# Later tables and a later row transpose in a mixture of 32 expert jobs on one core

## The chip, the cores and the metric

The kernel runs on one core of a Trainium2 chip. Its time is the device time of one execution in microseconds; the times of before are the median and the spread of three runs. Four engines matter here: TensorE (PE, matmuls), VectorE (DVE), ScalarE (ACT) and GpSimd (POOL, which here only issues indirect DMAs); SP issues the weight loads.

## The reference, cut to what matters

One encoder layer over 2048 tokens of 1024 floats: attention and retention share one input and one output projection, and then a mixture of 32 SwiGLU experts follows, of which each token uses two. Only the mixture is touched by the change:

```python
expert_id = grp[:, None] * MOE_EXPERTS_PER_GROUP + top_idx
...
h = jax.nn.silu(xblk @ w_gate[e]) * (xblk @ w_up[e])
return h @ w_down[e]
...
y = jnp.zeros((T + 1, D), f32).at[buf_tok].add(yb.astype(f32) * buf_w[:, None])[:T]
```

Every expert has a list of the tokens that chose it. A list may be longer than the space that the kernel gives it; then the rest has to be computed too.

## The kernel before, in words

Attention, retention, the output projection and the routing fill the first 1264 us. Routing sorts the experts by the length of their lists. Then 32 jobs follow, one for each expert, numbered here from 0. Jobs 0, 1 and 2 are light: a list of up to 128 rows. From job 3 on heavy jobs (128 rows and 32 or 64 more, the overflow of a long list) and light ones alternate, up to the last few.

A job has two parts. `gate_up` (lines 1559 to 1585) multiplies the job's rows by two weight matrices, in eight pieces of 128 x 1024 floats: four quarters q, each with a gate and an up piece. `down` multiplies the result by four more pieces. The weights are float32, and matmuls run on pairs of rounded parts: for each piece `fetch` (line 1469) takes the raw tile `mr` that SP loaded (512 KB, nine buffers), ACT makes the upper part `mh` (line 1484) and DVE the lower part `ml` (line 1485, raw minus upper). There are eight buffers of each part. A light job needs three matmuls of 512 columns for each 128 x 512 half of a piece, so 48 for `gate_up` and 24 for `down`; a heavy one needs two more for each three.

The rows of a job come by indirect DMAs on POOL's queue (`gather`, line 1502; tile `xg`, two buffers, four DMAs for 128 rows; `xgo` for the overflow), two jobs ahead. `rows` (line 1519) turns them: for all but jobs 0 and 31 by a DVE transpose (`turned`, line 1550; tile `xT`, line 1554), from which ACT makes `xhi` (line 1556) and DVE `xlo` (line 1557). `hidden` (line 1588) transposes a job's result on PE (line 1594) and splits it into `hhi` and `hlo`, for `down`.

The order in the source: while `gate_up` of job n runs, `between(q)` is called behind each of its four quarters. There the next side step is taken (q 0, 1 and 3), `hidden` of job n-1 is written down at q 1, the gathers of job n+2 at q 0, the rows of job n+1 at q 2. `down` of job n-1 comes behind `gate_up` of job n. A planner reads this order as priorities and fixes each engine's queue by its own simulated times; an instruction waits in its queue behind all before it. `high_priority` raises a block's priority, `issue_after` puts a block behind a named instruction on that engine's queue.

The side steps are the generators `units` (line 1247) and `completion` (line 1323), 21 steps in all, three in each job from job `SIDE` on. `units` makes the tables that are needed if a list overflows even its own overflow space: small DVE operations (tiles `u_...`), joined by a few small PE matmuls (lines 1260, 1282, 1287, 1294, 1316), each of which takes one of two PSUM buffers `pt`, as `hidden` does. `completion` makes the order in which finished tokens are normalized and stored (tiles `c_...`, `perm`); the first use of `perm` is in `loads` for job 11, called in job 13. The tables of `units` are read behind the last job.

Of the kernel before, what the change touches and what calls it, by code (L numbers as in the profile page):

```python
# [1443 lines left out]
R0 = 0.1  # L1444
W0 = 0.6
DG = 2
SIDE = 1
SQ = (0, 1, 3)
SP = 100
ORD = 1  # L1450
# [223 lines left out]
def experts(k):  # L1674
    nc, tc = k.nc, k.tc
    with ExitStack() as ctx:
        m = Moe(k, ctx)
        f = Final(k, ctx)
        order = job_order()
        jobs = []  # L1680
# [23 lines left out]
        def loads(n):  # L1704
            for c in range(NB):
                if DONE[c] == n:
                    C[c] = f.load(k.perm[:, c:c + 1])

        def column(n, step):

            for c in range(NB):
                if DONE[c] == n:
                    if step == 0:
                        with tc.issue_after(m.hi_at.ins):
                            f.square(C[c])
                    elif step == 1:
                        with tc.issue_after(m.lo_at.ins):
                            f.scale(C[c])
                    else:
                        f.store(C[c])  # L1720

        for n, X in enumerate(jobs):
            def between(q):
                if n >= SIDE and q in SQ:
                    with tc.high_priority(SP):
                        next(side, None)
                if q < 3:
                    if q and n < 31:
                        column(n - 3, q - 1)
                    elif n == 31:  # L1730
                        if q == 1:
                            loads(29)
                        column(28, q)
                if n == 31 and q == 1:
                    m.down(jobs[30], f.loads)
                    C[15] = f.load(k.perm[:, 15:16])
                    C[14] = f.load(k.perm[:, 14:15])
                elif n and q == (1 if n < 31 else 0):
                    with tc.high_priority(HID):
                        m.hidden(jobs[n - 1])  # L1740
                if q == 0:
                    for j in ([1, 2] if n == 0 else [n + 2]):
                        if j < 32:
                            m.gather(jobs[j])
                if q == 2 and n + 1 < 32:
                    if n < 31:
                        loads(n - 2)
                    if n:
                        m.rows(jobs[n + 1])
                    else:  # L1750
                        with tc.issue_after(k.split0.ins):
                            m.rows(jobs[1])
                if q == 3 and n < 31:
                    column(n - 3, 2)
            m.gate_up(X, between)
            if 0 < n < 31:
                m.down(jobs[n - 1], f.loads)
# [9 lines left out]
        n = nc.values_load(k.redo[0:1, 0:1], min_val=0, max_val=1)  # L1767
        with tc.For_i(0, n, 1):
# [3 lines left out]
            n = nc.values_load(k.nu[0:1, 0:1], min_val=0, max_val=64)  # L1772
# [154 lines left out]
```

## Time and profile before

| | us |
|---|---|
| median of three runs | 2099.15 |
| lowest and highest run | 2093.79, 2099.17 |
| profiled execution | 2083.01 |
| its span | 2081.2 |
| mean granted clock of PE | 0.969 |

The profiled execution is one run; between its span and its own time lie 1.8 us. It is 16.1 us (0.8%) below the median. Engine shares are of the span. Times in the rows count from the start of the span.

### The profile page before, as it was taken

The page shows a single profiled execution, that of the slowest core. Times are in us where ns is not written, and L with a number is a line of the kernel's source. Part 1 is how long each engine was busy: PE and PEld are TensorE (multiplying, and loading weights), DVE is VectorE, ACT ScalarE, POOL GpSimd, SP SyncE. Part 2 cuts the span into 40 slices and gives each one's busy share as a digit, 9 for nine tenths or more (in the row PEclk, how much of TensorE's full clock was granted, in tenths as well). Part 3 has the DMA queues.
Part 4 walks back from the last instruction along what each step waited for, and adds up shares of the span by engine and source line. Part 5 has one row for each costly group of instructions (what it writes and reads, how often), then busy time and mean ns, then how long its engine had stood idle before and what let it go on. Part 6 is the DMA issues. An engine that isn't in the chain of part 4 may idle for free.

```text
span 2081.2 us, 30110 instructions
## 1 busy us (share of the span) xinstructions
PE 1944.9 (93%) x9811; PEld 1543.9 (74%) x9811; DVE 1553.2 (75%) x3462; ACT 1122.7 (54%) x1915; POOL 673.7 (32%) x362
## 2 busy tenths in 40 slices
PE   7999999999999987789999996799999999999994
PEld 5788888878888875578887775577777677777673
DVE  7345446855565578987877767999988899998884
ACT  4244445634444454555454314676776787776663
POOL 0000000010000037421111105566867667875433
PEclk9999999999999998899999997799999999999997
DMA  6655344573675456463453455799999999998994
GB/s 201 193 153 171 117 135 144 178 242 129 195 213 167 137 160 215 128 203 132 156 183 111 138 223 182 254 304 296 338 343 320 319 339 349 353 344 302 338 316 117
DMA packets 241810, 459.61 MB, mean 221 GB/s; under 512 B 27376, under 2 KB 130160, under 8 KB 240624
## 3 DMA queue, kind: packets, MB, share of 16 engines
q1 hardware_dynamic: 224384, 401.53, 56.9%
q0 software_dynamic: 16976, 55.06, 9.8%
q8 instruction: 78, 1.28, 0.3%
q10 hardware_dynamic: 288, 1.05, 0.1%
q14 instruction: 84, 0.69, 0.1%
HBM read 365.81 MB, written 91.75 MB: 220 GB/s over the span
## 4 chain that ended last, share of the span: by engine, by line
PE 72%; DVE 9%; DMA 7%; issue 5%; SPq 2%; POOL 2%; ACT 2%; ACTq 0%; DVEq 0%; POOLq 0%
PE pa L63 7%; PE pa L62 7%; PE pa L64 7%; PE acc L63 7%; PE acc L62 7%; PE acc L64 7%; PE acc L72 4%; PE acc L74 3%; PE pS L350 3%; PE pS L351 3%; PE pT L382 2%; PE pF L62 2%; PE pF L64 2%; PE pF L63 2%; DMA wr<-in_w_in_dram 2%
## 5 line engine op out<-in xcount | busy, mean ns | idle before, releaser
L1485 DVE TENSOR_TENSOR ml<-mr,mh 128x1024 fp32r<-128x1024 f32 x376 | 446.5, 1214 | 38.6 <-ACT mh L1484 32.4
L1484 ACT ACTIVATE mh<-mr 128x1024 fp32r<-128x1024 f32 x376 | 385.5, 1055 | 124.0 <-PE acc L74 66.3
L1515 POOL DMA_INDIRECT xg<-XN,TA x120 | 270.0, 2250 | 64.3 <-issue 30.5
L352 DVE CUSTOM_DVE_ANT_0 p<-pS,dist 128x512 f32<-128x512 f32 (+1 forms) x320 | 188.0, 605 | 126.3 <-PE pS L351 118.5
L426 POOL TENSOR_TENSOR U<-U,r 128x512 f32<-128x512 f32 (+2 forms) x13 | 16.5, 1270 | 725.9 <-DVE r L40 623.9
L359 ACT ACTIVATE p<-p,nm 128x128 f32<-128x128 f32 (+15 forms) x128 | 153.9, 1203 | 111.8 <-DVE nm L358 111.5
L63 PE MATMUL acc<-ml,xhi 128*128 128x512 f32 x512 | 205.9, 403 | 5.0 <-DVE ml L1485 5.0
L64 PE MATMUL acc<-mh,xlo 128*128 128x512 f32 x512 | 206.2, 403 | 1.3 <-DVE xlo L1557 1.3
L62 PE MATMUL acc<-mh,xhi 128*128 128x512 f32 x512 | 204.0, 401 | 0.0
L54 ACT ACTIVATE ah<-pT 128x512 fp32r<-128x512 f32 (+2 forms) x176 | 85.4, 498 | 141.1 <-PE pT L382 99.6
L62 PE MATMUL pa<-xh,whi 128*128 128x512 f32 x384 | 152.9, 398 | 2.0 <-DVE nlam L633 2.0
L62 PE MATMUL pa<-whi,xh 128*128 128x512 f32 x384 | 151.8, 398 | 2.9 <-ACT whi L161 2.1
L63 PE MATMUL pa<-wlo,xh 128*128 128x512 f32 x384 | 153.1, 399 | 1.5 <-DVE nm L358 1.2
L64 PE MATMUL pa<-whi,xl 128*128 128x512 f32 x384 | 153.9, 401 | 0.0
L63 PE MATMUL pa<-xl,whi 128*128 128x512 f32 x384 | 151.8, 395 | 0.0
L64 PE MATMUL pa<-xh,wlo 128*128 128x512 f32 x384 | 151.6, 395 | 0.0
L350 PE MATMUL pS<-kst,qs 128*128 128x512 f32 (+1 forms) x320 | 123.5, 398 | 21.6 <-DVE cm L352 8.9
L162 DVE TENSOR_TENSOR wlo<-wr,whi 128x1024 fp32r<-128x1024 f32 x72 | 89.9, 1250 | 67.0 <-ACT whi L161 64.4
L55 DVE TENSOR_TENSOR al<-pT,ah 128x512 fp32r<-128x512 f32 (+2 forms) x176 | 97.5, 564 | 44.9 <-ACT ah L54 44.4
L62 PEld LDWEIGHTS acc<-mh,xhi 128*128 128x128 f32 x512 | 97.3, 190 | 31.8 <-ACT xhi L54 0.2
L161 ACT ACTIVATE whi<-wr 128x1024 fp32r<-128x1024 f32 x72 | 76.1, 1059 | 81.2 <-DMA wr<-in_w_in_dram 39.9
L63 PEld LDWEIGHTS acc<-ml,xhi 128*128 128x128 f32 x512 | 97.6, 191 | 28.9 <-DVE ml L1485 5.4
(536 smaller groups left out, 4912.5 us busy)
## 6 DMA issues: line engine op xcount, KB each, us to landing
mr<-in_expert_w_gate_dram SPq DMA_DIRECT2D x128, 512.0 KB
mr<-in_expert_w_up_dram SPq DMA_DIRECT2D x128, 512.0 KB
mr<-in_expert_w_down_dram SPq DMA_DIRECT2D x128, 512.0 KB
wr<-in_w_in_dram SPq DMA_DIRECT2D x72, 512.0 KB
vst<-VS SPq DMA_DIRECT2D x72, 256.0 KB
qs<-QS SPq DMA_DIRECT2D x128, 128.0 KB
st<-in_x_dram SPq DMA_DIRECT2D x16, 512.0 KB
VS<-st SPq DMA_DIRECT2D x32, 256.0 KB
```

The costliest lines, as they stand in the source:

```text
L54: nc.scalar.activation(hi, ps, AF.Copy)
L55: return nc.vector.tensor_sub(lo, ps, hi.bitcast(F32))
L62: nc.tensor.matmul(out, s_hi, m_hi, start=start, stop=False)
L63: nc.tensor.matmul(out, s_hi, m_lo, start=False, stop=False)
L64: nc.tensor.matmul(out, s_lo, m_hi, start=False, stop=stop)
L162: nc.vector.tensor_sub(lo, r, hi.bitcast(F32))
L350: nc.tensor.matmul(x, qs[0][:, m, 0, o:o + 128], ks[m][:, a0:a1], start=True, stop=False)
L352: nc.vector.tensor_tensor_reduce(p[:, a0:a1], x, tab[:, c0 + a0:c0 + a1], SLOPES[h], -3.0e38, OP.add, OP.max, accum_out=cm[:, n:n + 1])
L359: nc.scalar.activation(p[:, :nk], p[:, :nk], AF.Exp, bias=nm, accum_out=s0 if m == 0 else s1)
L1484: self.hi_at = nc.scalar.activation(hi, r, AF.Copy)
L1485: self.lo_at = nc.vector.tensor_sub(lo, r, hi.bitcast(F32))
L1515: nc.gpsimd.indirect_dma_start(out=xg[:, g * 256:(g + 1) * 256], out_offset=None, in_=v, in_offset=bass.IndirectOffsetOnAxis(ap=ix[:, g], ...
```

## The change

Two things move. The first side step is taken in job 3 and not in job 1; the 21 steps then end in job 9 and not in job 7. The rows of job 2 are written down behind the last quarter of job 1 and not behind its third, and all of that block stands behind `m.lo_at`, the DVE subtraction of the last weight piece that `gate_up` of job 1 fetched. The `loads` keep their place.

```diff
-SIDE = 1
+SIDE = 3
...
-                if q == 2 and n + 1 < 32:
-                    if n < 31:
-                        loads(n - 2)
-                    if n:
+                if q == 2 and n < 31:
+                    loads(n - 2)
+                if q == (3 if n == 1 else 2) and n + 1 < 32:
+                    if n == 1:
+                        with tc.issue_after(m.lo_at.ins):
+                            m.rows(jobs[2])
+                    elif n:
                         m.rows(jobs[n + 1])
```

## Rows read from the trace of the kernel before

**Rows 1.** The profile's page: busy time of each engine with its share of the span and its instructions, and the clock that PE was granted in 40 equal slices of 52 us, in tenths.

```profile
PE 1944.9 (93%) x9811; PEld 1543.9 (74%) x9811; DVE 1553.2 (75%) x3462; ACT 1122.7 (54%) x1915; POOL 673.7 (32%) x362
...
PEclk9999999999999998899999997799999999999997
```

**Rows 2.** PE in order of time: start, length, instruction, count, in brackets the idle time before it and what ended it. The last three lines are the end of `down` of job 1 and the first matmul of job 3.

```profile
1296.82 0.63 PE L62 MATMUL acc<-mh,xhi 128*128 128x512 f32 x2
1302.46 0.79 PE L63 MATMUL acc<-ml,xhi 128*128 128x512 f32 x1 [5.01 <-DVE ml L1485]
...
1306.03 0.63 PE L63 MATMUL acc<-ml,xhi 128*128 128x512 f32 x1
1306.46 0.63 PE L64 MATMUL acc<-mh,xlo 128*128 128x512 f32 x1
1317.90 0.60 PE L1282 MATMUL pt<-u_tri,u_w 32*128 32x32 f32 x2 [10.81 <-DVE u_w L1291]
...
1347.08 0.40 PE L63 MATMUL acc<-ml,hhi 128*128 128x512 f32 x1
1347.32 0.39 PE L64 MATMUL acc<-mh,hlo 128*128 128x512 f32 x1
1347.55 0.39 PE L62 MATMUL acc<-mh,xhi 128*128 128x512 f32 x1
```

**Rows 3.** Waits of all engines from 1325 us to the end: who waited for whom; us in total, times, longest.

```profile
ACT mh L1484 <- PE acc L74: 66.3, 55, 2.8
...
DVE fh L1620 <- DMA fh<-H,perm: 5.8, 1, 5.8
...
PE acc L63 <- DVE ml L1485: 3.7, 5, 1.8
```

**Rows 4.** Stretches: from and to, length, busy us (instructions) of each engine, granted clock of PE as a share of 2.4 GHz, DMA share, GB/s.

```profile
1290.00:1297.00 7.00, 7.00 (x31) 5.64 (x30) 2.15 (x2) 3.26 (x4) 5.52 (x4) 1.00 1.03 404
1297.50:1302.40 4.90, 0.00 (x0) 0.00 (x0) 3.16 (x4) 1.12 (x2) 2.31 (x3) 0.86 0.49 171
1302.40:1307.10 4.70, 4.63 (x10) 3.14 (x10) 4.70 (x7) 4.70 (x6) 4.09 (x3) 0.50 0.77 235
1307.10:1317.90 10.80, 0.00 (x0) 0.03 (x1) 10.80 (x14) 2.45 (x3) 9.89 (x4) 0.50 0.72 222
1317.90:1324.70 6.80, 6.67 (x19) 5.18 (x20) 5.12 (x12) 1.23 (x2) 5.28 (x6) 0.50 0.59 208
1324.70:1347.50 22.80, 22.80 (x99) 17.54 (x98) 19.62 (x31) 18.45 (x21) 5.89 (x5) 1.00 0.85 270
1347.50:1436.00 88.50, 88.28 (x403) 66.69 (x402) 84.58 (x118) 63.79 (x77) 53.66 (x21) 1.00 0.92 306
1480.00:1525.00 45.00, 45.00 (x201) 34.89 (x200) 40.71 (x40) 33.09 (x41) 34.94 (x13) 1.00 0.99 332
```

**Rows 5.** DVE in order of time, with the columns of rows 2.

```profile
1289.82 2.34 DVE L1485 TENSOR_TENSOR ml<-mr,mh 128x1024 fp32r<-128x1024 f32 x2
1299.24 2.01 DVE L1554 STREAM_TRANSPOSE xT<-xg 128x1024 f32<-128x1024 f32 x1 [7.08 <-DMA xg<-XN,TA]
...
1301.20 3.47 DVE L1485 TENSOR_TENSOR ml<-mr,mh 128x1024 fp32r<-128x1024 f32 x3
1304.60 0.13 DVE L1273 CAST u_ui<-u_u 32x1 int32<-32x1 f32 x1
...
1317.55 0.21 DVE L1279 COPY u_w<-u_u 32x128 f32<-32x128 f32 x1
...
1320.37 2.05 DVE L1554 STREAM_TRANSPOSE xT<-xg 128x1024 f32<-128x1024 f32 x1
```

**Rows 6.** DVE from 1264 to 1480 us, grouped by line and operation: count, busy us, mean ns of one, idle time before and its releaser. The last two are the largest and the smallest of the 72 groups of side steps (lines 1260 to 1429); the 72 come to 23.7 us.

```profile
L1554 DVE STREAM_TRANSPOSE xT<-xg 128x1024 f32<-128x1024 f32 x10 | 21.9, 2190 | 7.1 <-DMA xg<-XN,TA 7.1
L1557 DVE TENSOR_TENSOR xlo<-xT,xhi 128x1024 fp32r<-128x1024 f32 x9 | 10.9, 1210 | 0.0
...
L1596 DVE TENSOR_TENSOR hlo<-pt,hhi 128x512 fp32r<-128x512 f32 x8 | 5.4, 677 | 0.0
L1576 DVE SCALAR_TENSOR_TENSOR sg<-sg,wa,acc 128x512 f32<-128x512 f32 x7 | 5.1, 734 | 0.0
L1554 DVE STREAM_TRANSPOSE xT<-xgo 128x512 f32<-128x512 f32 x4 | 4.8, 1191 | 0.0
...
L1557 DVE TENSOR_TENSOR xov<-xT,xov 128x512 fp32r<-128x512 f32 x4 | 2.7, 685 | 0.1
...
L1406 DVE TENSOR_SCALAR c_sl<-i,c_d 128x128 bf16<-128x128 f32 x16 | 3.4, 278 | 0.0
...
L1334 DVE DVE_READ_ACCUMULATOR c_px<-P,posr 32x1 f32 x1 | 0.1, 70 | 0.0
```

**Rows 7.** POOL in order of time: start and length of what issues one gather DMA of a quarter of a job's rows. The second is the last of job 2.

```profile
1283.50 6.49 POOL L1515 DMA_INDIRECT xg<-XN,TA  x1 [0.30 <-issue]
...
1293.29 0.95 POOL L1515 DMA_INDIRECT xg<-XN,TA  x1 [0.30 <-issue]
...
1305.80 5.50 POOL L1515 DMA_INDIRECT xg<-XN,TA  x1 [0.31 <-issue]
```

**Rows 8.** Waits of SP's queue from 1255 us on, with the columns of rows 3.

```profile
SPq L1499 <- DVE ml L1485: 395.5, 264, 9.7
```

## The prediction

> **What bounds the kernel now.** I read the page first: PE is busy 93% of the span, and its clock row falls to 0.7 in the slices 25 and 26, from 1249 to 1353 us [rows 1]. That is where the jobs begin, and there the change works. Then PE in order of time. In the last quarter of job 1 it stands for 5.01 us on the lower part of a weight piece, runs the ten matmuls that are left, and stands for 10.81 us in front of line 1282, a matmul of the second side step [rows 2]. From 1325 us to the end it waits only 3.7 us for weights in all, and it is ACT that waits for PE to give a buffer back, 66.3 us [rows 3]: eight split pieces are normally ready ahead. So past 1325 us a microsecond won on PE is a microsecond of the kernel, as long as DVE and the transfers keep up.
>
> The stretches give the price of the two stops. PE is idle for 4.90 and 10.80 us in them, and after each it runs at half clock (0.50, that is 1.2 GHz) for 4.63 and 6.67 busy us before it is back at 2.4 GHz [rows 4].
>
> DVE in order of time says why it stood. Behind the sixth piece of job 1 its queue has the transpose of job 2's rows, and that waits 7.08 us for a gather; the last two pieces of job 1 stand behind it, though their upper parts are there. The second stop: the copy `u_w`, which line 1282 reads, comes at 1317.55, at the end of a row of tiny side operations with weight pieces between them [rows 5].
>
> **The change part by part.** All sums are made against the profiled execution: 2083.01 us, which is 16.1 below the median of the runs. What is won is subtracted from the median.
>
> *The transpose moved behind the last piece.* The two pieces that PE waits for go ahead of it: DVE is free at 1289.82 + 2.34 = 1292.16, a piece takes 1.13 (three from 1301.20 to 1304.60), so they are there at 1294.4 [rows 5], before PE asks for them at 1297.45. The stop of 5.01 goes [rows 2]. What is late next: the transpose still waits for the gather. Nothing of the gather moves, so I let it begin at 1299.24 again; it takes 1.93, and the first piece of job 0's `down` behind it is ready at 1299.24 + 1.93 + 1.13 = 1302.3. PE ends job 1 at 1297.45 + 10 x 0.235 = 1299.8 (0.235 is the spacing at 1347.08, 1347.32 and 1347.55; at half clock it is 0.43) [rows 2]. Two matmuls of the upper part can go ahead, 0.5, so PE still stands 2.1 here. If the planner puts that piece ahead of the transpose, it is 0; if the gather lands later, it is that much more.
>
> *The side steps moved two jobs.* Line 1282 is no longer in PE's queue in front of `hidden` of job 0: the 10.81 goes. With both stops the half clock goes too, half of 4.63 + 6.67 = 5.6 [rows 4]. The small PE matmuls (lines 1282 to 1316) cost the same two jobs later, so nothing is won on them.
> Gross: 5.0 + 10.8 + 5.6 = 21.4.
>
> *What DVE gives back before job 3.* In the second stop DVE was busy for all of 10.80 us [rows 4]; it worked ahead while PE stood. Without the stop it is the limit. From 1299.24 to the first piece of job 3 it has to do: the transpose 1.93; 16 pieces (4 of job 0's `down`, 8 of job 2, 4 of job 1's `down`) at 1.13, 18.1; `xlo` 1.1; two each of `sg` and `hlo`, 2.5; the rows of job 3, 1.9 + 1.1 + 1.1 + 0.6 with the overflow; the first piece of job 3, 1.1 [rows 5, 6]. That is 29.4: job 3 begins at 1328.6. PE for its part needs from 1302.3 on 24 + 48 + 24 matmuls less the two, 94 x 0.235 = 22.1, and two groups of `hidden` transposes, 0.9: 1325.3. So DVE costs 3.3 more. It is 0 if the rows of job 3 come when DVE is not short, and 5.4 if the planner takes the rows of job 4 ahead as it does now (2.05 at 1320.37) [rows 5]. Cross-check: job 3 begins at 1347.55 now; 18.9 earlier, of which some 2 are side matmuls only moved, agrees with 21.4 - 2.1 - 3.3 = 16.0 to within one.
>
> *What DVE gives back after it.* Now job 3 begins with eight pieces in hand; then it begins with one. From 1347.5 to 1436 DVE is busy 84.58 of 88.5, with side steps in it, and at 1480, when they are over, 40.71 of 45 [rows 4]. The side steps come to 23.7 us of DVE [rows 6]. Moved, jobs 3 to 6 get the first 12 of 21 steps, the light ones, and jobs 7 to 9 the rest. So DVE has a few us to spare in jobs 3 to 6 and is short in 7 to 9. PE loses between 0 (the reserve is built again) and 8 x 1.13 = 9.0 (it was needed whole); I take 3.5, nearer to 0 because the stretch has 3.9 to spare even with the side steps of now.
>
> *The issue_after.* It is a place in a queue, no instruction. What stands behind the transpose on DVE is `down` of job 0, counted above. On ACT `xhi` of job 2 waits with it, and the upper parts behind it; ACT has 1.12 busy of 4.90 there [rows 4], so it is not the later one. SP's queue waits for DVE to free raw tiles (395.5 us over the jobs) [rows 8], so two loads are issued 9 us sooner, behind the two pieces that go ahead; POOL gets buffers back at the same time as now. `loads` keep their place.
>
> Sum: 21.4 - 2.1 - 3.3 - 3.5 = 12.5. Profiled: 2083.0 - 12.5 = 2070.5; median: 2099.15 - 12.5 = **2086.6 us**.
>
> A rule against it: POOL took 0.95 for the last gather DMA of job 2, while DVE stood still, but 6.49 and 5.50 for others beside a busy DVE [rows 7]. In the changed kernel DVE subtracts until 1294.4, across that issue at 1293.29. The Trainium skill, "SBUF — State Buffer", section "Who interferes with whom", says that a DVE instruction with two inputs in SBUF contends with a GpSimd instruction that reads SBUF, and that the loser blocks for the whole instruction; it infers that writing descriptors does not suffer. The long issues here speak for the first, the inference for nothing lost. By the first the gather lands up to two subtractions, 2.3 us, later, and the sum would be 10.2 and 2088.9; by the inference it stays at 12.5.
>
> **The rivals.**
> *Nothing given back.* The planner finds another order, DVE does the pieces of `down` while it waits for the gather, the reserve comes back. For it: 4.8 us of DVE stand idle between 1294.4 and 1299.24, room for four pieces. Against: rows come ahead of `down` in the source. Gain 21.4 less up to 2: 19.5, 2079.6.
> *The transfers are the bound.* From 1297.5 to 1347.5 about 11.9 MB were moved (GB/s times length of the five stretches); at the 332 GB/s that the later jobs reach at a share of 0.99 [rows 4] this takes 35.9 us and not the 33 that I need, and with no raw tiles in hand nothing is left for later. Gain 50 - 35.9 - 2 (moved matmuls) - 9.0 (whole reserve) = 3.1, 2096.0. For it: shares near 1. Against: 404 GB/s were reached from 1290 to 1297, and the loads wait for buffers, not the other way [rows 4, 8].
> *Slower: gathers late at three jobs.* DVE's long busy time stretches POOL's issues (5.50) [rows 7], so the rows of jobs 3 and 4 land after DVE comes to them, too, and each stops PE as now: 3 x (5.0 + 2.3 of half clock) for jobs 2 to 4, and the whole reserve of 9.0 gone: 21.4 - 21.9 - 9.0 = -9.5, 2108.6. It decides if DVE waits for `xg` in three jobs. Against: after 1325 us DVE waits for no gather of rows, the one DMA wait it has is for `fh` [rows 3].
> *It doesn't do what it says.* If the planner still puts job 2's transpose where a needed piece stands behind it (now a piece of `down`) and wins only the side steps, it is the second stop alone: 10.8 + 3.3 - 3.3 - 3.5 = 7.3, 2091.9. This lies inside the range.
>
> **How the numbers follow.** My forecast, gain 7 to 17 (2082 to 2092): 0.55, the last rival within it. Nothing given back: 0.15. Transfers the bound or the reserve lost, gain 0 to 7: 0.21. Slower than now: 0.09. The runs of before spread by 5.4 us; 0.3% is 6.3 us, about what a measurement of this kernel can tell from no change. Faster by more than that: 0.55 + 0.15 + 0.03 = 0.73; within it 0.20; slower by more 0.07. The range takes in the first rival with the spread of the runs, 2077, and most of the second, 2098.
>
> **What would show it.** Right: no wait for line 1282; the pieces of job 1 at 1294.4 and job 2's transpose behind them, still with a DMA wait of some 5 us; PE at 1.00 from 1300 to 1330; job 3 at 1327 to 1332. DVE near 100% until job 9, and PE waits for `ml` there of 2 to 6 us. Wrong: half clock again behind a stop in front of `down` of job 0; a DVE wait for `xg` in job 3 or 4; job 3 at 1335 or later; or PE waits for `ml` above 9 us in jobs 3 to 9.

## The result and the profile after

| | before | after |
|---|---|---|
| median, us (5 runs each, beside each other) | 2093.79 | 2081.85 |
| lowest and highest | 2092.31, 2099.17 | 2069.81, 2083.36 |
| profiled execution, its span | 2083.01, 2081.2 | 2069.81, 2068.0 |
| mean granted clock of PE | 0.969 | 0.973 |

The ratio is 0.9919 with a 95% interval of [0.989, 0.9949]: 17.0 us less [10.7, 23.0]. Two later sets of the same pair gave 0.9943 [0.9911, 0.9975] and 0.9968 [0.9943, 0.9993], 11.9 and 6.7 us. (The ratios are worked out from the single runs; the medians of the table lie 11.9 us apart. One run of the last set, 2194.19 us at a granted clock of 0.834, was in a slower state and is left out.) The change makes the kernel faster. The three intervals have 10.7 to 11.9 us in common, so the sets by themselves do not show that the gain differs from one to the next; the profiles do show executions that differ, and that is most of what follows.

The page of after; the second and the last line answer to [rows 1]:

```profile
span 2068.0 us, 30117 instructions
PE 1939.0 (94%) x9811; PEld 1539.9 (74%) x9811; DVE 1551.5 (75%) x3462; ACT 1122.5 (54%) x1915; POOL 663.0 (32%) x362
...
PEclk9999999999999999889999997999999999999997
```

Busy times hardly move; the clock row has one slice below 0.9 at the beginning of the jobs (0.7, slice 25) where [rows 1] has two. That slice ends at 1292.5 us and its low clock (0.67 from 1256.7 to 1275, then 1.00) comes ahead of any stop treated here; the kernel before has the same in its slice 25 (0.64 from 1264 to 1282). Only the second of the two slices was the stops'. To compare executions I count from a common point. The jobs begin where POOL issues the gather of job 0 (line 1510): at 1264.1 us in the profile of before, at 1256.7 in after. These 7.4 us are none of the change's: up to that point the queues of the two kernels are the same, and in the eighteen profiles of this study the point lies anywhere from 1256.7 to 1272.4, at 1264.1 and 1269.2 in two profiles of the kernel before. So of the 13.2 us between the spans, 5.8 come from the jobs. Even this is within what two executions of one kernel differ by: from that point to the end of the span it is 817.1 and 828.4 us in two profiles of the kernel before, and 811.3, 810.0 and 821.0 in three of the changed one. So the change is read below from the first 260 us of the jobs, where the profiles of one kernel can be told apart wait by wait, and not from the spans. From here on "+30" means 30 us after that point.

The waits of PE in after from 1255 to 1600 us: who waited for whom, us in total, times, longest.

```profile
PE acc L62 <- ACT hhi L1595: 6.8, 2, 5.2
PE pt L1533 <- DMA xg<-XN,fia: 3.4, 1, 3.4
PE acc L64 <- DVE hlo L1596: 1.7, 1, 1.7
```

The two stops of [rows 2], 5.01 on a lower part of job 1 and 10.81 in front of line 1282, are gone. A new one of 5.2 has come: PE waits for ACT's `hhi`, the upper part of job 0's hidden rows. It is in front of `down` of job 0. PE in order of time, then DVE, then ACT, the columns as in [rows 2]:

```profile
1292.28 0.40 PE L64 MATMUL acc<-mh,xlo 128*128 128x512 f32 x1
1297.93 0.80 PE L62 MATMUL acc<-mh,hhi 128*128 128x512 f32 x1 [5.25 <-ACT hhi L1595]
...
1302.61 1.22 PE L64 MATMUL acc<-mh,hlo 128*128 128x512 f32 x2 [1.75 <-DVE hlo L1596]
```

```profile
1282.17 4.63 DVE L1485 TENSOR_TENSOR ml<-mr,mh 128x1024 fp32r<-128x1024 f32 x4
1294.29 2.01 DVE L1554 STREAM_TRANSPOSE xT<-xg 128x1024 f32<-128x1024 f32 x1 [7.49 <-DMA xg<-XN,TA]
1296.22 4.59 DVE L1485 TENSOR_TENSOR ml<-mr,mh 128x1024 fp32r<-128x1024 f32 x4
```

```profile
1296.34 1.06 ACT L1556 ACTIVATE xhi<-xT 128x1024 fp32r<-128x1024 f32 x1 [8.62 <-DVE xT L1554]
1297.30 0.58 ACT L1595 ACTIVATE hhi<-pt 128x512 fp32r<-128x512 f32 x1
```

DVE has all of job 1 ready at 1286.8 and then stands 7.49 us on job 2's gather. ACT's queue has `xhi` of job 2 next, which reads the transpose, and `hhi` of job 0 behind it: 0.58 us of work that needs nothing of job 2 waits 8.62 us in line. PE waits for that. DVE is hardly earlier: the four lower parts of `down` of job 0 stand behind the transpose there (1296.22), the first ready at about 1297.4, and the first matmul of `down` begins at 1297.93. By these rows (an estimate) DVE's queue alone would have held PE for some 4.4 us; ACT's adds the rest. The gather is late on POOL:

```profile
1274.87 0.95 POOL L1515 DMA_INDIRECT xg<-XN,TA  x1 [0.30 <-issue]
1276.12 6.31 POOL L1515 DMA_INDIRECT xg<-XN,TA  x1 [0.30 <-issue]
1282.74 4.90 POOL L1515 DMA_INDIRECT xg<-XN,TA  x1 [0.30 <-issue]
1287.94 0.94 POOL L1515 DMA_INDIRECT xg<-XN,TA  x1 [0.30 <-issue]
1289.18 0.94 POOL L1515 DMA_INDIRECT xg<-XN,TA  x1 [0.30 <-issue]
...
1292.92 0.94 POOL L1515 DMA_INDIRECT xg<-XN,TA  x1 [0.30 <-issue]
```

The first four are job 2's. Two of them take 6.31 and 4.90 us beside DVE's subtractions; from 1288, with DVE standing still, each takes 0.94. The stretches, columns as in [rows 4]:

```profile
1286.70:1294.30 7.60, 5.98 (x28) 4.57 (x26) 0.12 (x2) 1.01 (x1) 5.65 (x6) 1.00 0.93 358
1294.30:1304.30 10.00, 4.62 (x10) 3.22 (x11) 10.00 (x9) 6.25 (x8) 6.81 (x4) 0.59 0.36 106
1304.30:1331.60 27.30, 27.30 (x116) 21.61 (x116) 27.30 (x29) 20.89 (x25) 17.64 (x10) 0.96 0.93 320
1331.60:1420.00 88.40, 86.82 (x375) 66.06 (x374) 82.08 (x109) 62.11 (x75) 62.73 (x23) 0.98 0.94 318
```

DVE is idle in the first (0.12 of 7.60). Behind the stop the granted clock is 0.59 on average in the second, near the lower level of 1.2 GHz, and 0.96 in the third. The half clock that the forecast saw going came back behind the new stop.

### The profile page after: what moved, and what is told of

The parts are those of the page before. It is cut to its first block, busy times and chain, and to the rows that moved or that the text cites. A ratio compares the mean times of both kernels' runs of the same rounds, so it can differ in the third digit from the quotient of the medians.

```text
span 2068.0 us, 30117 instructions
## 1 busy us (share of the span) xinstructions
PE 1939.0 (94%) x9811; PEld 1539.9 (74%) x9811; DVE 1551.5 (75%) x3462; ACT 1122.5 (54%) x1915; POOL 663.0 (32%) x362
## 3 DMA queue, kind: packets, MB, share of 16 engines
q10 hardware_dynamic: 288, 1.05, 0.1%
## 5 line engine op out<-in xcount | busy, mean ns | idle before, releaser
L162 DVE TENSOR_TENSOR wlo<-wr,whi 128x1024 fp32r<-128x1024 f32 x72 | 90.6, 1260 | 64.3 <-ACT whi L161 62.8
L64 PEld LDWEIGHTS acc<-mh,xlo 128*128 128x128 f32 x512 | 96.7, 189 | 24.3 <-DVE xlo L1557 2.1
```

The lines of the kernel that those rows point to most:

```text
L64: nc.tensor.matmul(out, s_lo, m_hi, start=False, stop=stop)
L162: nc.vector.tensor_sub(lo, r, hi.bitcast(F32))
```

## The experiments

Two measures serve for all of them: the start, after the jobs begin, of the expert matmul before which 192 others lie (the first of job 3) and of the one before which 900 lie, called matmul 192 and matmul 900, and so for other numbers; and DVE's wait for a gather of rows, with the time at which it ended. The ratio is that of the timed runs to the kernel before on the same chip.

| run | ratio [95%] | wait of DVE, us, at | matmul 192 | matmul 900 |
|---|---|---|---|---|
| before, r1_before | 1.0, 1.0 [0.9978, 1.0022] | 7.1 at +35, 7.3 at +35 | 83.5, 83.3 | 258.8, 258.6 |
| changed: after | 0.9919 [0.989, 0.9949] | 7.5 at +38 | 69.3 | 249.6 |
| changed: r2_after | 0.9943 [0.9911, 0.9975] | 0.7 at +31 | 62.7 | 241.4 |
| changed: e15_after | 0.9968 [0.9943, 0.9993] | 7.3 at +37 | 69.5 | 249.8 |
| e1_side | 0.9951 [0.9917, 0.9985] | 4.4 at +31 | 67.6 | 246.2 |
| e2_rows | 0.9969 [0.9944, 0.9995] | 0.9 at +31 | 70.5 | 245.5 |
| e3_behind_down | 0.9944 [0.9911, 0.9977] | 4.0 at +39 | 65.2 | 245.6 |
| e4_gather_first | 0.9921 [0.989, 0.9951] | 5.4 at +47 | 65.3 | 245.9 |
| e5_before_gather | 0.9999 [0.997, 1.0027] | 6.4 at +46 | 82.6 | 257.9 |
| e6_both | 0.9908 [0.9873, 0.9942] | 6.5 at +53 | 65.8 | 246.3 |
| e8_own_order | 0.995 [0.9922, 0.9978] | 5.8 at +80 | 60.3 | 248.9 |
| e9_own_behind | 0.9897 [0.9865, 0.9929] | 6.1 at +82 | 59.7 | 245.2 |
| e14_best (e9 again) | 0.9937 [0.9913, 0.9961] | 5.4 at +103 | 59.6 | 246.7 |
| e10_side6 | 0.9989 [0.996, 1.0017] | 8.2 at +102 | 60.5 | 245.3 |
| e11_gaps | 1.0023 [0.9998, 1.0047] | 5.7 at +36, 7.1 at +271 | 68.5 | 249.8 |
| e12_own_gaps | 0.9976 [0.9951, 1.0001] | 7.0 at +85 | 59.8 | 247.3 |
| e13_gaps_two | 1.0035 [1.0011, 1.0058] | 5.6 at +36, 5.8 at +275 | 65.8 | 255.9 |

**The two kernels again, and each half of the change alone.** e1_side begins the side steps two jobs later and leaves the rows where they were; e2_rows is the reverse.

```
e1_side:                                  e2_rows:
-SIDE = 1                                 the change, but
+SIDE = 3                                 SIDE = 1
 if q == 2 and n + 1 < 32:  (as before)
```

> The kernel before once more, unedited. Two lengths are read from its trace: the first stretch, up to POOL's first gather of the jobs (1264.1 us in the first trace of before, 1256.7 in that of the changed kernel, though the queues up to there are the same), and the job stage, from that gather to the end of the span (817.1 before, 811.3 changed). Theory 'noise': the first stretch moves by several us from run to run whatever the kernel, here anywhere from 1250 to 1266, and the job stage is steady, 817 within 1. Rival 'the change reaches into the first stretch': it stays at 1264 within 2 here and at 1257 within 2 in every kernel with the changed order.

> The changed kernel once more, unedited. Theory 'noise': job stage 811.3 within 1, first stretch anywhere from 1250 to 1266, time ratio to before between 0.990 and 0.997. Rival 'the change reaches into the first stretch': first stretch 1257 within 2 and a ratio near 0.992.

> Only the side steps begin in job 3; the rows of job 2 stay at the third quarter of job 1. Theory 'renamed' (in the changed kernel the wait for job 2's gather stops PE all the same, one step later, through the split of job 0's result that stands behind job 2's rows on ACT): this part alone has nearly the whole gain of the job stage, 810 to 813; the stop of some 5 us on the lower part of a weight piece is there again. Rival 'both parts as predicted': without the move of the rows the first stop of 5.0 and its half clock of 2.3 stay, less the 2.1 that the move costs: job stage 5 longer than changed, 816.

> Only the rows of job 2 are moved; the side steps begin in job 1 as before. Theory 'renamed': the stop in front of line 1282 stays, the first stop is taken into it (one long stop instead of two), job stage 815 to 818. Rival 'both parts as predicted': 5.0 + 2.3 - 2.1 = 5.2 are won, job stage 812.

The difference in the first stretch is noise: it was 1269.2 in r1_before and 1270.8 in r2_after, both above the 1266 expected. The other half of that theory failed: the job stage of the kernel before was not steady within 1 us (828.4 after 817.1). So the forecasts of e1 and e2 by job stage (802.7 and 807.3 came, outside them all) decide nothing. In the jobs r2_after is another picture than after: the same kernel, the same queues, but the gather of job 2 comes in time.

```profile
1288.98 0.95 POOL L1515 DMA_INDIRECT xg<-XN,TA  x1 [0.30 <-issue]
1290.23 1.74 POOL L1515 DMA_INDIRECT xg<-XN,TA  x1 [0.30 <-issue]
1292.28 1.97 POOL L1515 DMA_INDIRECT xg<-XN,TA  x1 [0.30 <-issue]
1294.55 1.97 POOL L1515 DMA_INDIRECT xg<-XN,TA  x1 [0.30 <-issue]
```

```profile
1289.97 4.59 DVE L1485 TENSOR_TENSOR ml<-mr,mh 128x1024 fp32r<-128x1024 f32 x4
...
1301.62 2.28 DVE L1554 STREAM_TRANSPOSE xT<-xg 128x1024 f32<-128x1024 f32 x1 [0.73 <-DMA xg<-XN,TA]
```

The four issues end at 1296.5 (+25.7) in place of +32.2, beside the same subtractions, and matmul 192 comes 6.6 us sooner than in after. Neither half is worthless alone. e2_rows stops 6.29 at line 1282 in place of 10.81, since DVE, not held by the gather (0.9), gets to `u_w` sooner. In e1_side the gather is there at +31 already, and PE stops 0.95 on a weight piece, not the 5 expected, and 2.91 on `hlo`. By matmul 900 the two are 12.6 (e1) and 13.3 us (e2) ahead of the kernel before, the changed kernel 9.2 to 17.4, and the intervals of their ratios overlap: which half is worth more is not shown. The halves do not add; part of each hangs on when the gather lands.

**The transpose behind `down` of job 0** (e3_behind_down).

```
-                if q == (3 if n == 1 else 2) and n + 1 < 32:
+                if q == 2 and n != 1 and n + 1 < 32:
...
             if 0 < n < 31:
                 m.down(jobs[n - 1], f.loads)
+            if n == 1:
+                with tc.issue_after(m.lo_at.ins):
+                    m.rows(jobs[2])
```

> The changed kernel, with the rows of job 2 written down behind `down` of job 0, so that on ACT the upper part of job 0's hidden rows stands ahead of `xhi` of job 2 and on DVE `hlo` ahead of the transpose. Theory Q (what stops PE in front of `down` of job 0 is the place in ACT's and DVE's queues behind a transpose that waits for its gather): even if the gather lands as late as 35 to 38 us after the jobs begin, PE no longer waits there for `hhi` (5.2 in the changed kernel's first profile); the stop moves to the transposed rows of job 2 or vanishes; matmul 216 of the jobs at 68 to 72 us after their begin, ratio to before 0.990 to 0.995. Rival G (the gather itself is too late, wherever its transpose stands): PE stops just as long, only one group of matmuls later, in front of job 2; matmul 216 at 74 to 76 when the gather lands late, ratio as the changed kernel's, 0.992 to 0.996.

The wait for `hhi` of job 0 is gone although the gather is not in time (+39, DVE waits 4.0); PE still stands 2.86 us there, for `hlo`. Matmul 216 comes at 70.8, in the range expected by Q. DVE, then PE, of e3:

```profile
1291.36 9.19 DVE L1485 TENSOR_TENSOR ml<-mr,mh 128x1024 fp32r<-128x1024 f32 x8
1304.56 2.01 DVE L1554 STREAM_TRANSPOSE xT<-xg 128x1024 f32<-128x1024 f32 x1 [4.02 <-DMA xg<-XN,TA]
1306.49 0.65 DVE L1596 TENSOR_TENSOR hlo<-pt,hhi 128x512 fp32r<-128x512 f32 x1
```

```profile
1307.19 0.73 PE L64 MATMUL acc<-mh,hlo 128*128 128x512 f32 x2 [2.86 <-DVE hlo L1596]
```

The edit moves two queues at once: on ACT `hhi` comes ahead of `xhi`, and on DVE the four lower parts of `down` come ahead of the transpose, as `m.lo_at` is the last of them by then (eight pieces in a row here, four in after). So the places behind the waiting transpose were the stop in after; what ACT's place did by itself is not shown. `hlo`, which stands behind the transpose still, is what is left.

**Order of the gathers.** In both kernels POOL issues the four gathers of overflowing rows (for jobs 3 and 5) ahead of job 2's. e4_gather_first puts them behind job 2's in the changed kernel, e5_before_gather in the kernel before, e6_both joins e4 and e3.

```
+                        if j in (3, 5):
+                            with tc.issue_after(m.g_at.ins):
+                                m.gather(jobs[j])
...
+                            g = m.gather(jobs[j])
+                            if j == 2:
+                                m.g_at = g
```

> The changed kernel, with the gathers of the two lists that overflow (for jobs 3 and 5, four DMAs) put behind the gather of job 2 (four DMAs) in POOL's queue. Theory G (PE's last stop hangs on when POOL issues job 2's gather): its last issue ends some 13 us sooner than the 25.8 to 32.1 us after the jobs begin, DVE does not wait for `xg` of job 2, PE has no stop over 2 us in front of `down` of job 0, matmul 216 at 66 to 70 us after the begin and matmul 1200 at 311 to 316, as in the changed kernel's better profile (68.3 and 313.8), and no execution at 74.9; ratio to before 0.990 to 0.994. Rival D (DVE and the missing reserve set the pace until job 10, so what is won early is given back): matmul 216 at 66 to 70, but matmul 1200 at 318 to 322, ratio 0.993 to 0.997. Rival V (the gathers of the lists that overflow are needed soon, and late ones stop DVE in front of job 3): a DVE wait for `xgo` of 5 us or more in front of job 3, ratio 0.996 or above.

> The kernel before, with that order of the gathers alone. Theory G: the first stop (5.0 to 5.4 us on the lower part of a weight piece of job 1) goes, since the transpose in front of it waits for nothing; the stop in front of line 1282 stays (10.8, perhaps longer by the 5 that no longer come before it); matmul 216 at 82 to 86 us after the jobs begin (89.9 before), matmul 1200 at 323 to 327 (330.5 before), ratio to before 0.996 to 0.999. Rival Q (the place of the transpose in the queues sets the stop): the first stop stays at 3 or more, ratio 0.999 to 1.001. By both it is behind the run with the rows' move alone (0.9969) or beside it.

> The changed kernel with both edits: rows of job 2 behind `down` of job 0, and their gather ahead of those of the lists that overflow. Theory G: the gather is there long before, so the place of the transpose is worth nothing any more, and this equals the run with the gather's order alone within 0.2%. Theory Q: it equals the run with the rows behind `down` alone within 0.2%. If both hold for a part, it is the fastest of the four, matmul 216 at 64 to 68 and a ratio of 0.989 to 0.992. Rival D: no better than the changed kernel (0.992 to 0.995), though PE has no stop over 2 us before job 3.

All three remove DVE's wait for job 2, and in all three it comes back one job later, 5.4 to 6.5 us for job 3, whose gather now stands behind the others. Matmul 900 is at 245.9 (e4) and 246.3 (e6), as with the late gather of e3. For e4 the late sizes are rival D's (matmul 1200 at 318.3; G had 311 to 316), while the ratio is in G's range. e6 equals e4 within 0.2%, as G said, but its matmul 216, at 73.0, is later than the 64 to 68 that both edits together were to give. The wait for `xgo` of rival V came nowhere. e5 shows what such a wait costs where something is queued behind it. DVE and PE of e5:

```profile
1314.05 2.01 DVE L1555 STREAM_TRANSPOSE xT<-xg 128x1024 f32<-128x1024 f32 x1 [6.41 <-DMA xg<-XN,TA]
```

```profile
1321.56 0.60 PE L1282 MATMUL pt<-u_tri,u_w 32*128 32x32 f32 x2 [16.07 <-DVE u_w L1291]
```

The first stop goes, as G said, and its 5 us are added to the second: 16.07 for 5.01 + 10.81. The gain is nothing (0.9999; matmul 216 at 89.2, where G had 82 to 86). In the kernel before the side steps in the queue took whatever the gather gave.

**Overflow behind its own job's rows** (e8_own_order; e9_own_behind with e3's edit; e10_side6 with the side steps at job 6).

```
                 for g in range(n // 32):
+                    if idx is X.idx:
+                        at = nc.gpsimd.indirect_dma_start(out=xg[:, g * 256:(g + 1) * 256], ...
+                        continue
+                    with k.tc.issue_after(at.ins):
...
e10_side6:
-SIDE = 3
+SIDE = 6
```

> The changed kernel, with each overflow list gathered behind its own job's rows on POOL: the gathers of jobs 1, 2 and 3 come first (twelve DMAs), the two of job 3's overflow behind them, job 5's later still. Theory P (what is lost in front of jobs 2 and 3 is DVE time spent waiting for gathers that POOL issues late beside DVE's subtractions; afterwards DVE is busy without a break, so every us it waits stays lost): DVE waits less than 1 us for `xg` in jobs 1 to 3, against 7.5 in the changed kernel, 5.4 and 6.5 where job 3's gather became the late one; DVE is at 10.0 of 10 from 11 to 60 us after the jobs begin; matmul 216 at 66 to 69 and matmul 1200 at 311 to 314.5 after the begin, where the five kernels with a wait of 4 to 6 lie at 317 to 319; ratio to before 0.988 to 0.992. Rival D (a floor that DVE's work and the transfers set whatever the gathers do): matmul 288 at 91.5 to 92.5 and matmul 1200 at 317.5 to 318.5 again, though DVE waits for no gather. Rival O (the overflow rows of job 3 are late instead): a DVE wait of 3 or more for `xgo`, matmul 1200 at 317 or later.

> The same order of the gathers, with the rows of job 2 behind `down` of job 0 as well. Theory P: with no late gather the place of the transpose is worth nothing, so matmul 1200 is within 1.5 us of the run with the gathers' order alone and the two ratios within 0.2%. Theory Q (the place counts by itself, because `hhi` and `hlo` of job 0 come sooner): 2 to 3 us sooner at matmul 108 and still so at matmul 1200.

> That order of the gathers, with the tables' side steps begun at job 6 in place of job 3. The forecast took it that DVE is short until job 3 and the reserve of split pieces comes back slowly afterwards; DVE is at 10.0 of 10 in nearly all stretches from 35 to 120 us after the begin. If that is what bounds the jobs 3 to 5 (theory D'): without the side steps' 3.9 to 5 us there, matmul 384 comes 2 to 4 us sooner than with them at job 3, and matmul 1200 within 1 us of it or up to 2 sooner. Rival (PE bounds there, and a side step costs the same wherever it stands): matmul 384 sooner only by the small PE instructions moved, under 1 us, and matmul 1200 the same within 1 us. The ratio to before is 0.986 to 0.992 by both; slower than the run with the steps at job 3 only if the tables then come too late for the lists that need them.

Now no gather is late for jobs 1 to 4, and up to there theory P is right: in e9 DVE is busy without a break for 64.2 us, PE is at full clock but for a moment, and matmul 192 comes at 59.7.

```profile
1277.30:1341.50 64.20, 61.12 (x262) 47.46 (x261) 64.20 (x65) 47.50 (x53) 57.41 (x18) 0.99 0.88 313
```

Behind it the late gather is there again, at +80, +82 and +102:

```profile
1347.88 2.01 DVE L1559 STREAM_TRANSPOSE xT<-xg 128x1024 f32<-128x1024 f32 x1 [5.80 <-DMA xg<-XN,TA]
```

```profile
1347.65 2.02 DVE L1559 STREAM_TRANSPOSE xT<-xg 128x1024 f32<-128x1024 f32 x1 [6.09 <-DMA xg<-XN,TA]
```

```profile
1367.23 2.00 DVE L1559 STREAM_TRANSPOSE xT<-xg 128x1024 f32<-128x1024 f32 x1 [8.22 <-DMA xg<-XN,TA]
```

The three lines are e8, e9 and e10. In e8 the first side steps are queued there, and PE stops 7.42 us at line 1282 again; in e10 it stops 7.60 in a `down`, and 3.3 us more near +305 on DVE's `sg` and `hv`. So P's price (a wait is lost) holds and its promise (matmul 1200 at 311 to 314.5) fails: e8 has 321.3, e9 317.0. e9 is 0.6 us ahead of e8 at matmul 108 and 4.3 at matmul 1200, so its own forecasts (no difference by P, 2 to 3 us throughout by Q) both failed. e10 is 2.4 us ahead of e8 at matmul 384, as D' said, but 5.5 behind at matmul 1200. The wait walks.

**Why POOL is late.** e11_gaps puts a tiny DVE instruction with one input in SBUF behind every second weight subtraction from job 1 on, 64 in all (NG is 128). The last comes at +280, in job 11; the "jobs 0 to 5" of what was expected is a miscount. e13_gaps_two is its control, with two inputs; e12_own_gaps is e11's edit in e9.

```
             self.lo_at = nc.vector.tensor_sub(lo, r, hi.bitcast(F32))
+            self.nf += 1
+            if self.nf <= NG and self.nf % 2 == 0:
+                with k.tc.issue_after(self.lo_at.ins):
+                    nc.vector.tensor_scalar(self.gap, self.gap, 0.0, 127.0, op0=OP.max, op1=OP.add)
e13_gaps_two:
+                    nc.vector.tensor_sub(self.gap, self.gap, self.gap)
```

> The changed kernel, with a tiny DVE instruction (32x1, one input in SBUF) behind every second weight subtraction of jobs 0 to 5; 64 of them at about 0.07 make 4.5 us more of DVE. Theory S (POOL's gather issues are shut out by runs of subtractions, which read two inputs in SBUF, and get in beside any DVE instruction with one such input, however short): the issues of job 2's gather take at most 2.5 to 3.5 each in place of 6.3 and 4.9, its last issue ends by 27 us after the jobs begin (32.1 in the changed kernel's first profile), and DVE waits for it under 2 us; no POOL issue before 100 us takes over 4; DVE has no wait for a gather over 2 us before 330 us; matmul 900 at 241 to 244 (245 to 249 in the kernels with one late gather, 241.4 in the one profile without). Ratio to before 0.989 to 0.993. Rival B (what makes an issue long is POOL's own work or the DMA queue, and it only happens to end with a DVE instruction): issues of 5 to 9 us as before, one DVE wait of 4 to 8 us, matmul 900 at 247 to 252 with the added DVE time, ratio 0.993 to 0.998.

> The same tiny instructions in the run with the overflow gathered behind its own job's rows and the rows of job 2 behind `down` of job 0. Theory S: no issue over 4 before 100 us, the DVE wait of 6.1 in front of job 5 gone, matmul 216 at 66 to 68, matmul 900 at 239 to 242, ratio 0.986 to 0.990: the fastest of all. Rival B: the late gather stays where it was (a DVE wait of 4 to 8 at 75 to 85 us after the begin), matmul 900 at 246 to 250, ratio 0.990 to 0.994.

> The control to the first of these three: the same tiny instruction in the same places of DVE's queue, but with two inputs in SBUF (a subtraction, 32x1). Theory S: it opens nothing, the issues take 4.5 to 9 us beside runs of subtractions, and DVE waits once for 4 to 8 us, matmul 900 at 247 to 252. If a gap between instructions is all that POOL needs (theory S'), it is as good as the instruction with one input, with issues of 3.5 at most. Rival B: both alike and both long.

As a remedy it fails: the waits stay (e11 and e13 have a second one after +270), and all three ratios are above those of the same kernels without. The profile of e11, of its fastest run, does not show where that time goes: matmul 900 comes at 249.8, as in after. As a probe it shows something. POOL and DVE of e11:

```profile
1285.06 2.81 POOL L1523 DMA_INDIRECT xg<-XN,TA  x1 [0.30 <-issue]
1288.17 3.12 POOL L1523 DMA_INDIRECT xg<-XN,TA  x1 [0.30 <-issue]
1291.60 5.01 POOL L1523 DMA_INDIRECT xg<-XN,TA  x1 [0.30 <-issue]
```

```profile
1286.93 0.13 DVE L1493 TENSOR_SCALAR gap<-gap 32x1 f32<-32x1 f32 x1
...
1290.40 0.13 DVE L1493 TENSOR_SCALAR gap<-gap 32x1 f32<-32x1 f32 x1
...
1293.39 0.13 DVE L1493 TENSOR_SCALAR gap<-gap 32x1 f32<-32x1 f32 x1
...
1295.72 0.13 DVE L1493 TENSOR_SCALAR gap<-gap 32x1 f32<-32x1 f32 x1
```

The issues end at 1287.87, 1291.29 and 1296.61: 0.94, 0.89 and 0.89 after the begin of the first, second and fourth of the tiny instructions, which is the length of an undisturbed issue. The third let nothing in, and the second has a rival: `sg`, which reads one input in SBUF and one in PSUM, begins 0.06 us behind it. Over fifteen profiles without such an edit, from +5 to +330, 344 gather issues took over 2.3 us, and 269 of them ended 0.80 to 1.05 us after DVE began an instruction with at most one input in SBUF or fell idle; at random times it would be 44. So most long issues end at an opening in DVE's work. Whether the opening must have one input the control did not settle: in e13 the issues of 4.29 and 5.04 end 0.9 after a two-input tiny instruction, but an instruction with one SBUF input, or the end of DVE's work, lies 0.07 and 0.14 us behind it.

**The best order beside the changed kernel.**

> The run with the overflow gathered behind its own job's rows and the rows of job 2 behind `down` of job 0, once more and longer, beside the changed kernel. If the wait for a gather only walks (theory W: DVE waits once for 4 to 8 us, in whichever job, and that is lost), it is as good as the changed kernel with a well-timed gather and better than it with a late one: matmul 900 at 244 to 246 after the jobs begin, ratio to before 0.990 to 0.994, 0 to 0.3% below the changed kernel's. If the order is worth more than that (theory P), ratio 0.987 to 0.990 again, and over 0.3% below the changed kernel's.

> The changed kernel as it is, for the comparison on one chip. Ratio to before 0.991 to 0.995 by both theories; DVE's wait for the gather of job 2 is either under 1 (matmul 900 at 241 to 242 after the jobs begin) or 5 to 7.5 (matmul 900 at 247 to 250).

On one chip: 0.9937 [0.9913, 0.9961] and 0.9968 [0.9943, 0.9993], medians 2073.54 and 2079.84. That is 0.3% in favour of the order. The intervals overlap, but both carry the spread of the kernel before; run against run, the six of the order (2071.7 to 2075.7) and the eleven of the changed kernel (2070.9 to 2095.2) have means 7.7 us apart, with an interval of about 4 to 12 from resampling the runs. So on this chip the order is the faster one. e6 and e9 had medians of 2073.09 and 2073.58 on other chips, the changed kernel 2081.85, 2079.91 and 2079.84. Where the order wins is not shown: matmul 900 at 246.7 lies within the changed kernel's own 241.4 to 249.8. The ratio is theory W's and not P's, the distance to the changed kernel lies on the bound between the two, and the wait is still there, as W says.

## Why the prediction was right and where it was wrong

**The size.** 12.5 us were forecast, 0.60%; 17.0, 11.9 and 6.7 were measured, and each of the three intervals but the last, whose upper end is 11.9, holds it. The time itself, 2086.6, was 4.8 us too high, which puts the measured 2081.85 just below the 2082 to 2092 of the forecast. That came from the base: the median of three runs, 2099.15, against medians of 2087.2 to 2094.7 of the kernel before in all later sets. The step that failed there is "What is won is subtracted from the median"; from the 2093.79 beside which the change was measured the same sum gives 2081.3. That this is so near is luck: in the three profiles of the changed kernel the lead over the kernel before at matmul 900 is 9.2, 17.4 and 9.0 us, and the terms of the sum were wrong both ways.

**The first stop.** Right: the last pieces of job 1 are ready at +30.1 (forecast 1294.4, which is +30.3), and PE does not wait for them.

**The second stop.** Right: no wait for line 1282 there; e5 and e2 show it as a stop of its own that only the side steps' move removes whole. Gross 21.4 with some 2 of moved small matmuls also stands: in e9, where PE stands only 0.57 us at `down` of job 0, matmul 192 is 23.8 us sooner than before.

**PE in front of `down` of job 0: 2.1.** This is the step of the mechanism that failed. It was reckoned on DVE's queue alone, at full clock and for a gather at +35.2. What it cost: from matmul 84 to matmul 120 after takes 18.9 us, e9 9.3, r2_after 12.3. So the term is 9.7 with a late gather and 3.0 with one in time. Of the 9.7, 6.4 are waits (5.25 for `hhi`, 1.75 for `hlo`, less the 0.57 of e9), and 3.2 are left for the half clock behind them; of the 3.0 it is 1.5 and 1.5. The forecast put no half clock behind this stop: it counted all 5.6 as won. On ACT it said "so it is not the later one", from ACT's share of busy time (1.12 of 4.90, [rows 4]), which says nothing about what stands behind the one instruction that waits. `hhi` did, and it was the later one, by some 0.5 us over DVE's lower parts.

**The gather "at 1299.24 again".** The forecast held it at +35.2 in every execution. It came at +37.6, +30.8 and +37.4 in the three profiles of the changed kernel: twice some 2.4 us later, about the 2.3 of the rule that was weighed and left out of the sum, and once 4.3 sooner, which no term foresaw.

**DVE before job 3: 3.3.** Too high: from matmul 120 to matmul 192 all three profiles of the changed kernel and e9 take the same 17.4 us, and PE waits for nothing there (27.30 busy of 27.30 in after), so the term is 0. The lead at job 3, 18.9 on the trace (1347.55 less 1328.6), was measured as 14.2, 20.8 and 13.9: two errors of opposite sign, the 9.7 and the 3.3, cancel in part.

**After job 3: 3.5 and the moved small matmuls.** Right in size: from matmul 192 to 900 the lead falls by 5.0, 3.4 and 5.0. "DVE near 100% until job 9" and "PE waits for `ml` of 2 to 6" were wrong in their place: PE's listed waits from 1325 to 1600 us are 1.6 for `hhi`, none for `ml`, and DVE is at 82.08 of 88.40 from 1331.6.

**The rule weighed against it.** The Trainium skill, "SBUF — State Buffer", section "Who interferes with whom", has a DVE instruction with two SBUF inputs contend with GpSimd's reads, and infers that writing descriptors does not suffer. In these runs 0.95 becomes 1.97 or 4.9 to 9.4 us beside subtractions. That speaks against the inference for these gathers; but each of them also reads its row numbers from a tile in SBUF (`ix`), so the first rule may be at work and not the writing of descriptors, and no run separates the two. I had put the price at the last issue of job 2 (2.3); that one took 0.94, since DVE stood still by then. The price was at the two before it.

**The rivals.** "Gathers late at three jobs" had the right mechanism and the wrong bound: in the profiles of both kernels up to +330, DVE waits once. While it stands, POOL issues at 0.94 each and gets ahead for the next jobs. "Transfers the bound" fell for these jobs (share 0.93, 320 GB/s from 1304.3 to 1331.6, with PE busy throughout). "Nothing given back" fits r2_after up to matmul 900 (17.4) and no other. "Doesn't do what it says" had its condition in part, since lower parts of `down` do stand behind the transpose, but both stops went and the lead at matmul 900 is above its 7.3 in all three profiles.

What stays open: from matmul 1200 to 1800 kernels of either kind take 144 to 161 us, 148.8 and 160.3 in the two profiles of the kernel before; PE waits there for weights at about +390 and +450 in some executions. Much of the spread between runs may come from this and from the first stretch; neither was tried. Open is also what makes an issue on POOL long in one execution and short in the next, and in which share of the executions the gather is late.

## What to carry to other kernels

When a stop is removed, follow every queue that the moved instruction stands in: an engine that is 20% busy can be the late one, if one waiting instruction heads its queue. A wait that comes from one engine's rate (here POOL's issues beside DVE) walks to the next user when the order is changed, so look for it two and three jobs on before counting it as won. And take the base of an absolute forecast from as many runs as there are: the median of three lay 4 to 12 us above those of the later sets, about as much as this change is worth.

## What the hardware showed that I had not expected

The length of a gather issue on POOL has two forms with the same neighbours: 6.31 and 4.90 in two of the changed kernel's profiles, 1.74 and 1.97 in the third, beside the same run of subtractions. The two forms go with matmul 900 at 249.6 and 249.8, and at 241.4. Why there are two is not known.

The first 1264 us, in which nothing was changed, begin the jobs up to 15.7 us apart.

64 tiny DVE instructions, 4.5 us at 0.07 each from begin to begin, came with ratios 0.4 to 1% above those of the same kernels without them (e11 1.0023 against 0.9919 to 0.9968, e12 0.9976 against 0.9897 and 0.9937, whose interval meets that of e12). A small buffer and a memset came with them, and which of these it is wasn't tried.
